# The input projection of two token groups by seven block products in place of eight

## The chip, the core and the metric

The kernel runs on one core of one Trainium2 chip. A core has TensorE (PE; matmuls into PSUM, with a weight load, PEld, ahead of each), VectorE (DVE), ScalarE (ACT), GpSimd (POOL) and SyncE (SP), which issues nearly all DMAs of this kernel. Each engine works through its own queue in order. The metric is device time in microseconds; the median of the runs before is 2421.81 us (2421.06 to 2422.79, three runs).

## The reference

One layer of a decoder step on 2048 prompt tokens and 64 sample tokens (8 sequences of 8), model width 1024, float32:

```
h    = rmsnorm(x, norm_mix_w)
rq, rk, rv, rg, hq, hf, hi, hg = split(h @ w_in)          # 8 parts of 4 heads x 128 columns
A: rq, rk rotated; retention with a fixed decay per head  (chunks, running 128x128 state)
B: f = lb + (1-lb)*sigmoid(hf);  k = 1-f;  q = silu(hq);  S_t = diag(f_t) S_(t-1) + k_t v_t^T;  o_t = S_t^T q_t
o    = concat(head_rmsnorm(o_A)*silu(rg), head_rmsnorm(o_B)*silu(hg))
x    = x + o @ w_out
x    = x + square(relu(rmsnorm(x, norm_ffn_w) @ w_up)) @ w_down       # width 4096
y    = rmsnorm(x, final_norm_w)
```

The outputs are y for both token sets and the final states of both head groups.

## The kernel before

The tokens are worked on in three groups (`GROUPS`): group one has the 64 sample tokens and 512 prompt tokens (576 columns, worked on in two pieces of 288), groups two and three have 768 prompt tokens each (two pieces of 384). For each group in turn the mixing runs (`mix`, then `out_proj`); after that the three groups go through the feed-forward (`ffn`).

Every float32 operand is held as two parts, `hi` (rounded to the fast matmul type) and `lo` (the rest), and a product is three matmuls: hi x hi, hi x lo, lo x hi. A weight tile is 128 x 1024. Loaded raw, it is cast on ACT into `hi` (L273), and DVE subtracts to get `lo` (L287, `second_part`). `weight` keeps a fixed number of tiles ahead of use (`self.ahead`, 2). There are `NPART` = 5 buffers for each part and `NRAW` = 4 raw ones. Group one's weights, from the fifth on, are also written out as parts (`keep`), and groups two and three load the two parts ("p" entries of `plan_stream`) in place of casting again.

Mixing takes one head of each kind at a time, four times a group. `project` makes the forget, query, rotary query and rotary key blocks by `proj`, with a weight block stationary and tokens moving: 8 blocks of the contraction, 3 part products, 2 pieces (L347). DVE and ACT take each result out of PSUM, scaled by the reciprocal norm. `values` makes values and gates of both kinds with 128 tokens stationary and 512 weight columns moving (L793), and holds four weight tiles at once. `mixer` then does the chunkwise recurrence of that head. It does not run its steps at once. It puts them on an agenda with due times in ticks (`at`, `later`); `proj` ticks once per part product, and `values` ticks too, so the mixer's steps of one head lie between the projection matmuls of the next. Weight sums of the feed-forward are made meanwhile by `plan_sums`, on its own tick list (`side`), eight sets in each of groups two and three, with raw tiles and DVE (L1401).

The feed-forward is already done by seven block products in place of eight (`PRODUCTS`, `T_SUMS`): a matrix product is cut into 2 x 2 blocks, and sums of weight blocks (S1 to S4, made ahead and kept in DRAM) and of activation blocks (T1 to T4) take the place of one product. `product` does one of them, 2 x 4 x 3 = 24 matmuls (through `matmul`, L1369), and `up` adds the results together from PSUM, with four two-bank PSUM tiles in turn (`two_banks`). The mixing stage has two such tiles (pool `pj`) and four single banks (`mm`).

Temporaries are 128 x 768 tiles from one pool (`get`, `NSLAB` = 43) and six more for loads (`load`). Tiles are handed out as their last readers finish. A scheduler orders each engine's instructions by due place and readiness, except where `keep_in_program_order` fixes it. A second, general form of the kernel (`fast` False) is built behind a branch and runs only if decays reach too far.

Of the kernel before, what the change touches and what calls it, by code (L numbers as in the profile page):

```python
# [15 lines left out]
P = 128  # L16
# [13 lines left out]
NSLAB = 43  # L30
NLD = 6
NRAW = 4
NPART = 5
# [26 lines left out]
N_KEPT = W_OUT0 + 4  # L60

# [13 lines left out]
PRODUCTS = (("A11", "B11"), ("S2", "T2"), ("A12", "B21"), ("S3", "T3"), ("S1", "T1"), ("A22", "T4"), ("S4", "B22"))  # L75
EARLY, LATE = (("A12", "B21"), ("S4", "B22")), (("S2", "T2"), ("S3", "T3"), ("S1", "T1"), ("A22", "T4"))
# [127 lines left out]
class Kernel:  # L204
    def __init__(self, tc, I, O, fast):
        self.tc, self.nc, self.I, self.O, self.fast = tc, tc.nc, I, O, fast
        self.tag = "f" if fast else "g"
        self.agenda, self.n_at, self.now = [], 0, 0
# [40 lines left out]
    def weight(self, i):  # L249
        n = len(self.stream)  # L250
        while self.w_next < min(i + 1 + self.ahead, n):
            j = self.w_next
            e = self.stream[j]
            if e[0] == "p":

                self.wts[j] = tuple(self.wp.tile([P, WT], F32R, tag=tag, name=tag, bufs=NPART) for tag in ("hi", "lo"))
# [3 lines left out]
                self.w_load = max(self.w_load, j + 1)  # L260
                continue
            while self.w_load <= j or j >= W_UQ0 and self.w_load <= j + 2 and self.w_load < n:
                if self.stream[self.w_load][0] == "p":
                    break
                k = self.w_load
                raw = self.raws[k] = self.wp.tile([P, WT], F32, tag="raw", name="raw", bufs=NRAW)
                e = self.stream[k]
                self.fetch(raw, self.sums[e[1]] if e[0] == "s" else self.I["w"][e[1]])
                self.w_load += 1
            raw = self.raws.pop(j)  # L270
            hi = self.wp.tile([P, WT], F32R, tag="hi", name="hi", bufs=NPART)
            lo = self.wp.tile([P, WT], F32R, tag="lo", name="lo", bufs=NPART)
            self.nc.scalar.copy(hi, raw)  # L273
            self.wts[j] = (hi, lo)
            self.second[j] = raw
            if j < 4:
                self.second_part(j)
            else:
                self.later(4, self.second_part, j)
# [3 lines left out]

    def second_part(self, j):
        if j in self.second:
# [3 lines left out]
    def plan_stream(self):  # L289
# [16 lines left out]
        mixing()  # L306
        mixing()
# [6 lines left out]
    def next_weight(self):  # L314
# [3 lines left out]
        if N_MADE <= i < N_KEPT:  # L318
# [5 lines left out]
    def keep(self, parts, kept):  # L324
        for part, k in zip(parts, kept):
            self.nc.sync.dma_start(k, part.bitcast(F32))

# [1661 lines left out]
```

## Time and profile before

| | us |
|---|---|
| median of the runs | 2421.81 |
| the profiled execution | 2421.02 |
| its span | 2419.2 |
| mixing of group one, from its first projection | 6.5 to 267.5 |
| mixing of group two / group three | 334 to 657 / 723 to 1046 |
| feed-forward | 1111 to the end |

The profile is of one execution. Its page gives busy times of each engine, the granted TensorE clock and DMA share in 40 slices, the chain of work that ended last, and groups of instructions by line. A table by stage gives, for each stretch, its length and the busy time of each engine. The chain of waits names, in order of time, what the next step waited for. The stage limits above are the times at which the line of the projection matmuls changes in the timeline.

### The profile page before, as it was taken

The page shows a single profiled execution, that of the slowest core. Times are in us where ns is not written, and L with a number is a line of the kernel's source. Part 1 is how long each engine was busy: PE and PEld are TensorE (multiplying, and loading weights), DVE is VectorE, ACT ScalarE, POOL GpSimd, SP SyncE. Part 2 cuts the span into 40 slices and gives each one's busy share as a digit, 9 for nine tenths or more (in the row PEclk, how much of TensorE's full clock was granted, in tenths as well). Part 3 has the DMA queues.
Part 4 walks back from the last instruction along what each step waited for, and adds up shares of the span by engine and source line. Part 5 has one row for each costly group of instructions (what it writes and reads, how often), then busy time and mean ns, then how long its engine had stood idle before and what let it go on. Part 6 is the DMA issues. An engine that isn't in the chain of part 4 may idle for free.

```text
span 2419.2 us, 37190 instructions
## 1 busy us (share of the span) xinstructions
PE 2399.0 (99%) x14650; PEld 2312.9 (96%) x14650; DVE 1597.4 (66%) x2014; ACT 1148.9 (47%) x1847; POOL 206.6 (9%) x230
## 2 busy tenths in 40 slices
PE   9999999999999999999999999999999999999998
PEld 8998898899899998899999999999999999999997
DVE  6555654443564443547868998766988887679886
ACT  6555543344543443435545555444544364445443
POOL 5222111211102101200000000000000000000000
PEclk9999999999999999999999999999999999999999
DMA  7777676556566655558768666766755557675542
GB/s 272 249 244 247 209 276 224 194 218 244 185 212 226 252 214 205 214 169 274 256 216 306 210 208 196 247 216 206 267 182 175 170 169 266 208 234 182 190 167 89
DMA packets 191966, 525.39 MB, mean 217 GB/s; under 512 B 21155, under 2 KB 62883, under 8 KB 191782
## 3 DMA queue, kind: packets, MB, share of 16 engines
q1 hardware_dynamic: 191638, 522.90, 63.0%
q8 instruction: 117, 1.92, 0.3%
q14 instruction: 67, 0.55, 0.1%
q10 hardware_dynamic: 144, 0.02, 0.0%
HBM read 389.14 MB, written 132.39 MB: 216 GB/s over the span
## 4 chain that ended last, share of the span: by engine, by line
PE 91%; DVE 3%; ACT 2%; issue 2%; POOL 1%; DMA 1%; DVEq 0%; ACTq 0%; POOLq 0%
PE pf L1369 27%; PE pj L1369 26%; PE pj L347 20%; PE pjv L793 11%; PE mm L1213 1%; PE mm L1215 1%; PE mm L1221 1%; PE mm L1358 1%; PE mm L990 1%; DVE slab L945 1%; PE mm L1143 1%; POOL slab L949 1%; PE mm L904 1%; DVE slab L974 0%; PE mm L838 0%
## 5 line engine op out<-in xcount | busy, mean ns | idle before, releaser
L273 ACT CAST hi<-raw 128x1024 fp32r<-128x1024 f32 x392 | 412.6, 1053 | 614.7 <-PE pf L1369 237.7
L1369 PE MATMUL pf<-slab,hi 128*128 128x384 f32 (+1 forms) x2768 | 652.0, 321 | 0.0
L1369 PE MATMUL pj<-slab,hi 128*128 128x384 f32 (+1 forms) x2608 | 617.8, 322 | 0.0
L287 DVE TENSOR_TENSOR lo<-raw,hi 128x1024 fp32r<-128x1024 f32 x392 | 481.7, 1230 | 127.0 <-ACT hi L273 122.5
L1369 PEld LDWEIGHTS pf<-slab,hi 128*128 128x128 f32 x2768 | 480.0, 188 | 0.1
L347 PE MATMUL pj<-slab,hi 128*128 128x384 f32 (+1 forms) x2304 | 477.3, 324 | 0.4 <-ACT hi L273 0.4
L1369 PEld LDWEIGHTS pj<-slab,hi 128*128 128x128 f32 x2608 | 453.6, 188 | 0.0
L1369 PE MATMUL pf<-slab,lo 128*128 128x384 f32 (+1 forms) x1384 | 443.1, 320 | 0.0
L1369 PE MATMUL pj<-slab,lo 128*128 128x384 f32 (+1 forms) x1304 | 418.9, 321 | 0.0
L347 PEld LDWEIGHTS pj<-slab,hi 128*128 128x128 f32 x2304 | 383.8, 188 | 4.1 <-issue 1.4
L793 PE MATMUL pjv<-hi,slab 128*128 128x512 f32 x1024 | 349.8, 402 | 0.0
L347 PE MATMUL pj<-slab,lo 128*128 128x384 f32 (+1 forms) x1152 | 281.5, 325 | 1.0 <-DVE lo L287 1.0
L1369 PEld LDWEIGHTS pf<-slab,lo 128*128 128x128 f32 x1384 | 260.1, 188 | 0.0
L1369 PEld LDWEIGHTS pj<-slab,lo 128*128 128x128 f32 x1304 | 245.0, 188 | 0.0
L793 PEld LDWEIGHTS pjv<-hi,slab 128*128 128x128 f32 x1024 | 192.6, 188 | 36.6
L793 PE MATMUL pjv<-lo,slab 128*128 128x512 f32 x512 | 200.8, 392 | 0.0
L347 PEld LDWEIGHTS pj<-slab,lo 128*128 128x128 f32 x1152 | 198.3, 188 | 1.5 <-DVE lo L287 1.5
L1460 ACT CAST slab<-slab 128x768 fp32r<-128x768 f32 (+1 forms) x192 | 145.7, 779 | 79.2 <-DVE slab L1471 53.9
L1464 DVE TENSOR_TENSOR slab<-slab 128x768 fp32r<-128x768 f32 (+1 forms) x192 | 166.4, 886 | 18.3 <-PE pf L1369 6.2
L793 PEld LDWEIGHTS pjv<-lo,slab 128*128 128x128 f32 x512 | 96.7, 189 | 15.8
L1401 DVE TENSOR_TENSOR raw<-raw 128x1024 f32<-128x1024 f32 x64 | 104.6, 1634 | 0.8
L1230 DVE SCALAR_TENSOR_TENSOR S<-S,mm 128x128 f32<-128x128 f32 x60 | 17.2, 286 | 111.7 <-PE mm L1221 102.2
(236 smaller groups left out, 2304.7 us busy)
## 6 DMA issues: line engine op xcount, KB each, us to landing
raw<-w SPq DMA_DIRECT2D x264, 512.0 KB, 4.5
slab<-fu SPq DMA_DIRECT2D x64, 384.0 KB, 5.1
fu<-ld SPq DMA_DIRECT2D x60, 384.0 KB, 4.1
ld<-x SPq DMA_DIRECT2D x32, 384.0 KB, 3.7
ld<-fin SPq DMA_DIRECT2D x28, 384.0 KB, 4.7
slab<-fu SPq DMA_DIRECT2D x32, 288.0 KB, 4.6
fu<-ld SPq DMA_DIRECT2D x30, 288.0 KB, 3.0
fres<-slab SPq DMA_DIRECT2D x16, 384.0 KB, 3.5
```

What stands on the lines that cost most here:

```text
L273: self.nc.scalar.copy(hi, raw)
L287: self.nc.vector.tensor_tensor(out=lo, in0=self.second.pop(j), in1=hi.bitcast(F32), op=ALU.subtract)
L347: self.nc.tensor.matmul(pj[:, i, :T2], w, a[:, c0:c1], start=j == 0 and q == 0, stop=j == n - 1 and q == 2)
L793: nc.tensor.matmul(dst, a[:, s:s + C], ww, start=kb == 0 and q == 0, stop=kb == KB - 1 and q == 2)
L904: nc.tensor.transpose(ps[:, j * P:(j + 1) * P], src[:, c], self.ident)
L945: nc.vector.tensor_tensor_scan(out=bb[:, c], data0=self.ones, data1=lf[:, c], initial=0.0, op0=ALU.mult, op1=ALU.add)
L949: nc.gpsimd.tensor_tensor(out=dd[:, n0:T].rearrange("p (n m) -> p n m", m=C), in0=b3, in1=b3[:, :, C // 2 - 1:C // 2].to_broadcast([P, n, ...
L990: nc.tensor.matmul(ps[:, j * P:(j + 1) * P], k[:, cols[c]], q[:, cols[c]], start=True, stop=True)
L1369: self.nc.tensor.matmul(*a, **k)
L1401: self.tc.keep_in_program_order(nc.vector.tensor_tensor(out=x[into], in0=x[a], in1=x[b], op=op))
L1460: self.nc.scalar.copy(hi[:, :g.T], B[name][:, :g.T])
L1464: self.nc.vector.tensor_tensor(out=lo[:, :g.T], in0=B[name][:, :g.T], in1=hi.bitcast(F32)[:, :g.T], op=ALU.subtract)
```

## The change

Group one and the feed-forward keep their matmuls. In groups two and three the input projection is done by seven block products for eight, twice per head:

- forget, query, rotary query and rotary key together are one 512-column output (`project_blocks`). Output columns are halved (forget and query / rotary query and key), as are the contraction and the tokens (384). Each of seven calls of `product` is 24 matmuls of 384 columns, weights stationary.
- values and gates together are another (`values_blocks`). Tokens are halved into trios of chunks, the output into values and gates. Each of seven calls of `product_t` is 3 x 4 x 3 = 36 matmuls of 256 columns, tokens stationary.

The sums of weight blocks for both are made during group one by `plan_in_sums`: 16 sets of four half tiles, summed on POOL, stored by DMA. `keep_blocks` writes group one's weight parts out in block form, for three of four blocks. `norm_blocks` takes the place of `norm_in` for groups two and three: it loads the activation blocks, weighs them on POOL, sums and splits them. Per head six weight tiles are loaded as kept parts and eight as raw sums, which are cast (`first_part`, five ticks later) and subtracted (`second_part`, nine ticks later). The fast form has 45 slabs, 6 raw tiles and 3 buffers of each part (`SIZES`); before, it was 43, 4 and 5. Group one's values are looped by weight tile (`values_direct`), so one tile at a time is held. Gate tiles are overwritten with the head outputs (`b["slabs"]`), and the outputs of the first three heads go to DRAM and back (`keep_heads`, `fetch_heads`).

```diff
+SIZES = {True: (45, 6, 3), False: (43, 4, 5)}
+FIRST = (("A11", "B11"), ("S4", "B22"), ("A12", "B21"), ("S2", "T2"), ("S3", "T3"), ("S1", "T1"), ("A22", "T4"))
 def weight(self, i):
...
+            if e[0] == "s" and j < self.n_sums:
+                self.later(5, self.first_part, j)
+                self.later(9, self.second_part, j)
+            else:
+                self.first_part(j)
...
+        def mixing_blocks():
+            for p in range(H):
+                for part in "PV":
+                    key = ("i", p, part)
+                    self.stream += [("s" if name[0] == "S" else "p", key + (name,)) for name, _ in (FIRST if part == "P" and not p else PRODUCTS)]
...
+    def plan_in_sums(self, start, each):
...
+        def make(x, name, a, op, b, into):
+            self.tc.keep_in_program_order(nc.gpsimd.tensor_tensor(out=x[into][:, :HALF], in0=x[a][:, :HALF], in1=x[b][:, :HALF], op=op))
...
+            if self.fast:
+                self.plan_in_sums(40, 40)
             self.mix(gs[0])
...
+    def norm_blocks(self, g):
...
+        for v, t0, t1 in ((0, 0, 40), (1, 84, 134)):
+            for j, name in enumerate(("B11", "B21", "B22", "B12")):
+                t = t0 + 7 * j
+                self.later(t, load, v, name)
+                self.later(t + 9, square, v, name)
+                self.later(t + 12, weigh, v, name)
+                if name != "B12":
+                    cut(t + 18, v, name)
+            for j, name in enumerate(("T3", "T2", "T1", "T4")):
+                self.later(t1 + 6 * j, self.block_sum, g, B[v], name)
+                cut(t1 + 6 * j + 4, v, name)
...
+    def project_blocks(self, g, p, b):
...
+        a = bank()
+        self.product(g, parts(a), "B11")
+        p1 = copied(a)
...
+            u = bank()
+            self.product(g, parts(u), "T2")
+            u2 = added(u, p1)
+        self.product(g, parts(a), "B21", False)
+        z = self.get()
+        nc.vector.tensor_tensor(out=b2(z), in0=a, in1=wide(g.rs, 0), op=ALU.mult)
+        gated(z, 0, False)
...
+        d = bank()
+        self.product(g, parts(d), "T3")
+        u3 = added(d, u2)
+        c = bank()
+        self.product(g, parts(c), "T1")
+        turned(added(c, u3), 1)
...
+        self.product(g, parts(d), "T4", False)
+        turned(added(d, u2), 0)
+        if p:
+            self.product(g, parts(c), "B22", False)
+            gated(added(c, u2), 1, True)
+
+    def product_t(self, g, ps, op, first=True):
+        hi, lo = self.next_weight()
+        for tb in range(TRIO):
+            for kb in range(KB // 2):
+                ah, al = (self.pair(g, s)[:, kb % 2, tb * C:(tb + 1) * C] for s in g.ops[kb // 2][op])
+                cols = slice(kb * 256, (kb + 1) * 256)
+                for j, (t, w) in enumerate(((ah, hi), (ah, lo), (al, hi))):
+
+                    self.nc.tensor.matmul(ps[:, tb * 256:(tb + 1) * 256], t, w[:, cols], start=first and kb == j == 0 and tb != 1,
+                                          stop=kb == KB // 2 - 1 and j == 2, skip_group_check=True)
+                self.tick()
...
+        if fast:
+            late = 13 if g.blocks else 0
...
+            at(4 + late, reaches)
+            at(15 + late, both_decays)
+            at(20 + late, both_decayed)
...
+            t = 92 if g.blocks else 96 if n0 else 84
+            outs(t)
```

`values_blocks` goes through the same seven products with `product_t` and takes each result out of PSUM in the same order; `gated` and `turned` are the gate and rotary steps on a result, partly on POOL.

More of the change, by code (lines that the diff above doesn't have):

```diff
@@ L282, in weight, with load_raws, first_part @@
         return self.wts[i]
+    def load_raws(self, j):
+        last = j if j < W_UQ0 else j + 2 if j >= self.n_sums else j + 1 if self.fast else j
+        if j < self.n_sums and self.stream[j][0] == "p" and not self.fast:
+            return
+        for k in range(j, min(last + 1, len(self.stream))):
+            e = self.stream[k]
+            if e[0] == "p" or k < self.w_load:
+                continue
+            raw = self.raws[k] = self.wp.tile([P, WT], F32, tag="raw", name="raw", bufs=self.n_raw)
+            self.fetch(raw, self.sums[e[1]] if e[0] == "s" else self.I["w"][e[1]])
+            self.w_load = k + 1
+    def first_part(self, j):
+        if j in self.first:
+            self.nc.scalar.copy(self.wts[j][0], self.first.pop(j))
     def second_part(self, j):
+        self.first_part(j)
         if j in self.second:
@@ L400, in build @@
             self.ahead = 2
-            self.wts, self.second, self.kept = {}, {}, {}
+            self.wts, self.first, self.second, self.kept = {}, {}, {}, {}
             self.blocks = deque()
```

356 lines of the change are left out of this document (312 added, 44 removed).

## The prediction

> **What bounds the kernel now.** I read the page first (busy shares, granted clock, chain), then the stage table, then the pace of matmuls inside each stage.
>
> ```profile
> span 2419.2 us, 37190 instructions
> PE 2399.0 (99%) x14650; PEld 2312.9 (96%) x14650; DVE 1597.4 (66%) x2014; ACT 1148.9 (47%) x1847; POOL 206.6 (9%) x230
> PEclk9999999999999999999999999999999999999999
> PE 91%; DVE 3%; ACT 2%; issue 2%; POOL 1%; DMA 1%; DVEq 0%; ACTq 0%; POOLq 0%
> ```
>
> TensorE is busy 99% of the span at full clock and carries 91% of the chain. Since a busy PE need not be at its peak, the stage table is checked next (columns: stretch, its length, busy us of PE, PEld, DVE, ACT, POOL, clock, DMA share, GB/s). Group one mixes until 267.5, groups two and three in 334:657 and 723:1046; the feed-forward starts at 1111.
>
> ```profile
> core 0: us, PE busy (x) PEld busy (x) DVE busy (x) ACT busy (x) POOL busy (x), PEclk, DMA share, GB/s
> 6.50:66.00 59.50, 57.14 (x341) 50.25 (x342) 39.27 (x49) 40.33 (x65) 30.82 (x36) 1.00 0.77 276
> 66.00:267.50 201.50, 201.06 (x1289) 179.52 (x1288) 105.32 (x196) 111.21 (x253) 49.06 (x66) 1.00 0.66 227
> 334.00:657.00 323.00, 321.50 (x1820) 294.68 (x1819) 139.11 (x208) 128.80 (x298) 55.43 (x50) 1.00 0.61 224
> 657.00:723.00 66.00, 66.00 (x397) 65.93 (x396) 43.37 (x57) 34.22 (x58) 4.04 (x4) 1.00 0.57 193
> 723.00:1046.00 323.00, 321.50 (x1819) 294.62 (x1818) 139.33 (x208) 128.91 (x298) 55.15 (x50) 1.00 0.61 223
> 1111.00:1470.00 359.00, 359.00 (x2693) 358.90 (x2692) 304.45 (x363) 192.94 (x239) 0.00 (x0) 1.00 0.74 244
> 1470.00:1938.00 468.00, 468.00 (x2704) 468.00 (x2703) 366.87 (x395) 219.95 (x252) 0.00 (x0) 1.00 0.63 205
> ```
>
> In both stages that the change rewrites, PE idles 1.5 us in 323. DVE stands at 43%, ACT at 40%, DMA at 61%. So time there is the sum of matmul durations, and a matmul taken away shortens the span, as long as what comes with it stays hidden.
>
> The matmuls concerned, by shape (L347 is the projection with weights stationary, and 768 of its 2304 belong to the output projection; L793 is the values and gates, a quarter of it group one's):
>
> ```profile
> L793 PE MATMUL pjv<-hi,slab 128*128 128x512 f32 x1024 | 349.8, 402 | 0.0
> L347 PE MATMUL pj<-slab,hi 128*128 128x384 f32 x1536 | 336.5, 337 | 0.0
> L793 PE MATMUL pjv<-lo,slab 128*128 128x512 f32 x512 | 200.8, 392 | 0.0
> L347 PE MATMUL pj<-slab,lo 128*128 128x384 f32 x768 | 197.6, 338 | 0.0
> ```
>
> The means (402, 337 ns) overlap, so the pace comes from unbroken runs: one stretch of the feed-forward (288 columns), two pieces and two head marks of the chain of waits (384 and 512 columns), and one run of the timeline (128 columns).
>
> ```profile
> 1197.30:1470.00 272.70, 272.70 (x2047) 1.00 0.72 237
> ```
> ```profile
> 378.77 0.91 PE mm L990 x6
> 396.15 6.83 PE pjv L793 x30
> 423.50 22.90 PE pj L347 x132
> 457.76 0.91 PE mm L990 x6
> ```
> ```profile
> 69.62 1.91 PE L838 MATMUL mm<-ld,slab 128*64 128x128 f32 x16
> ```
>
> 288 columns: 272.7/2047 = 133.2 ns. 384: 22.90/132 = 173.5. 512: 6.83/30 = 227.7. Slopes are 0.420 and 0.423 ns a column, so the three lie on one line of about 12 ns plus 0.42 a column. The 128-column run is off it at about 109 ns (1.91 us less one 0.27 us duration, over 15 steps). One head lasts 457.76 - 378.77 = 79.0 us.
>
> **The change, part by part.** *Forget to keys.* A head had 4 blocks x 8 x 3 x 2 = 192 matmuls of 384 columns and gets 7 x 24 = 168 of the same shape. 24 x 173.5 = 4.16 us a head, 8 heads: -33.3.
>
> *Values and gates.* 6 x 8 x 3 = 144 of 512 columns (32.8 us) become 7 x 36 = 252 of 256 columns. Nothing in the trace has 256 columns. The nearest rows are 288 (133 ns, upper end) and 128 (109 ns, lower end). The line gives 133.2 - 32 x 0.42 = 120 ns; I take it, since 288 lies on the line and is 32 columns away. 252 x 120 = 30.2, so -2.5 a head and -20.2 in all. At 133 the new form costs 33.5 (+0.8 a head, +6); at 109 it costs 27.5 (-42). PE in all: -53.5, between -27 and -75.
>
> The Trainium skill ("TensorE: Matmul & The Clock Gate", Back-to-back issue gap) gives columns/2.4 GHz + 2.5 ns, an estimate of 109 ns here, and by it the sum would be 22 us lower. The trace disagrees: 133.2, 173.5 and 227.7 against 122.5, 162.5 and 215.8, so the rows decide.
>
> *Group one: weight sums and kept blocks.* 16 sets add 64 POOL sums of 512 columns and 128 DMAs of 256 KB. POOL rows (the second at 512 columns):
>
> ```profile
> L975 POOL TENSOR_TENSOR slab<-slab 128x768 f32<-128x768 f32 x8 | 14.8, 1850 | 4.4 <-ACT slab L962 4.4
> L895 POOL TENSOR_TENSOR ld<-ld,slab 128x512 f32<-128x512 f32 x8 | 8.2, 1050 | 11.8 <-PE mm L838 8.9 <-DMA ret_so<-ld 3.0
> ```
>
> 64 x 1.05 = 67 us on a POOL busy 80 of 261: hidden. The bytes are tighter: 33.6 MB over 640 of 672 ticks (249 us) is +135 GB/s, and kept parts fall from 8 to 6 pairs of 1 MB a head (-32). 227 + 135 - 32 = 330, and the row's 227 at share 0.66 means 344 when full: 96%. At the start it is over: 276 + 135 + stores of the first four weights. Weights are fetched two ahead (some 13 us), which absorbs most. Cost 0 (cover holds) to 12 (the start's surplus of about 7 MB, 21 us of DMA time, less the 3 MB that the rest can make up); I take 3, near the cover.
>
> *Operands of groups two and three.* 14 splits for 8, 8 block sums, and 14 POOL products of 1.85 us, in out_proj where POOL is at 4 of 66 us and DVE at 43. Sums are read only from the fourth product on. Cost 0 to 5; 1.
>
> *Weight stream.* A head reads 6 kept pairs (1 MB each) and 8 sums (0.5 MB): 10.5 MB for 8.4. With the spilled heads that is about 13 MB a group more: 224 x 323 = 72 MB becomes 85 MB in 296 us, 287 GB/s, where 224/0.61 = 367 is full: 78%. Only 3 part buffers remain, so a pair is issued when the product three back ends, and has two products, 2 x 4.16 = 8.3 us bare (10.3 us with the mixer between). Landing times (us, last column) of those pairs now:
>
> ```profile
> lo<-fw11lo SPq DMA_DIRECT2D x2, 512.0 KB, 11.7
> hi<-fw20hi SPq DMA_DIRECT2D x2, 512.0 KB, 9.6
> lo<-fw19lo SPq DMA_DIRECT2D x2, 512.0 KB, 9.4
> hi<-fw28hi SPq DMA_DIRECT2D x2, 512.0 KB, 9.1
> hi<-fw12hi SPq DMA_DIRECT2D x2, 512.0 KB, 8.8
> lo<-fw27lo SPq DMA_DIRECT2D x2, 512.0 KB, 8.8
> lo<-fw5lo SPq DMA_DIRECT2D x2, 512.0 KB, 8.4
> hi<-fw6hi SPq DMA_DIRECT2D x2, 512.0 KB, 3.2
> ```
>
> Seven of 46 listed exceed 8.3 us, by 7.7 us together; two reads of 48 kept pairs would give about 8. On SP the waiting pair holds back sum loads, which have slack. Cost 0 to 16; I take 5, as most products have the mixer between.
>
> *Evacuations.* The DVE rows:
>
> ```profile
> L287 DVE TENSOR_TENSOR lo<-raw,hi 128x1024 fp32r<-128x1024 f32 x392 | 481.7, 1230 | 127.0 <-ACT hi L273 122.5 <-DMA raw<-fsd01S 2.9
> L690 DVE TENSOR_TENSOR slab<-pj,slab 128x768 f32<-128x768 f32 x16 | 15.3, 955 | 35.4 <-PE pj L347 35.4
> L754 DVE TENSOR_TENSOR slab<-slab 128x768 f32<-128x768 f32 x16 | 15.0, 940 | 3.9 <-POOL slab L753 3.9
> L974 DVE TENSOR_TENSOR slab<-slab 128x768 f32<-128x768 f32 x8 | 13.8, 1722 | 23.1 <-ACT slab L963 23.1
> ```
>
> A head gains 11 adds from PSUM (10.5 us), rotary in halves (3.9) and 8 second parts (9.8), and loses 7 operations (6.4): +17.8. DVE goes from 34 of 79 to 52 of 72 us, 72%. ACT gains 8 casts of about 1.05 and two copies: 31 to 41 us, 57%. Both stay below PE. But project_blocks and values_blocks turn over two PSUM pairs only: each product's pair is wanted again one product later, so an evacuation has 4.16 - 0.96 = 3.2 us of room, 112 times. The feed-forward has DVE at 78 to 85% without a PE wait, with four pairs. Cost 0 (as there) to 56 (each late by half a microsecond); I take 6, one hand-off in 18 late by a microsecond, since 72% is below the feed-forward's load.
>
> *Fewer part buffers in the feed-forward.* Five become three, so a cast starts when the product three back ends, not five. In group one a product lasts 24 x 0.133 = 3.2 us: two of them, less cast and second part (1.05 + 1.23), leave 4.1 us. Behind a waiting cast in ACT's queue stand copies out of PSUM, which wait no longer than one product's end. A late second part in the timeline, with its cast:
>
> ```profile
> 1451.18 1.05 ACT L273 CAST hi<-raw 128x1024 fp32r<-128x1024 f32 x1 [1.42 <-issue]
> 1458.35 2.35 DVE L287 TENSOR_TENSOR lo<-raw,hi 128x1024 fp32r<-128x1024 f32 x2
> ```
>
> 1458.35 - 1452.23 = 6.1 us of lag, 2 more than is left. This happens at the end of the stage, where DVE work bunches. Cost 0 to 10 (five weights 2 us late); 3. Groups two and three have 6.0 us of room: nothing.
>
> *Sum.* 2421.0 (the profiled execution: span 2419.2 and 1.8 around it) - 53.5 + 3 + 1 + 5 + 6 + 3 = 2385.5. The median of the runs is 0.8 above that execution: 2386.
>
> **The rivals.**
> 1. All cover holds, as in the stages above where PE never waits: 2421.8 - 53.5 = 2368. For it: the stage table. Against: three of the five covers are thinner than anything in this trace.
> 2. The 256-column pace is 133 ns, because a weight load per 256 columns binds: 26 us less gain, 2412. For it: loads double in number per column. Against: 109 ns in the 128-column run.
> 3. The pace is 109 ns: 2364. Against it: three points on one line.
> 4. Group one is paced by DMA: 12 for 3, 2395. For it: 96% of what the rows show.
> 5. Slower: DVE misses the PSUM hand-off. L974 takes 1722 ns where the same shape takes 940 (L754), and it runs beside a POOL operation of the same size (L975, 1850). The change puts more POOL work (gating, sums, weighing) beside DVE. A block of up to 0.9 us in front of the evacuations eats into the 3.2 us. It decides from 0.48 us lost per hand-off (53.5/112); at 0.6 us the time is 2421.8 - 53.5 + 67 + 12 of the other waits = 2447. Against it: POOL is busy 17% of these stages, so few hand-offs meet it.
>
> The Trainium skill ("SBUF — State Buffer", SBUF: two separate sides) has this as an exclusive lock: a DVE operation with two SBUF inputs and a GpSimd operation that reads SBUF block one another for the whole instruction. The trace agrees in kind (1722 against 940). By it PSUM-sourced adds, with one SBUF input, are delayed only by what stands ahead of them in the queue.
>
> **How the numbers follow.** Forecast 0.54, rival 1 0.12, rival 2 0.10, rival 3 0.04, rival 4 0.08, rival 5 0.12. A measurement of this kernel tells about 0.2% (5 us) from no change. Rival 5 is split 0.03 within that and 0.09 slower; the rest is faster, 0.88. The forecast's own range is 2370 to 2400. The range 2366 to 2414 takes in rivals 1, 2 and 4 for the most part and leaves out rival 3 and rival 5, with some of rival 2: about 0.81.
>
> **What would show it.** Right: heads of groups two and three about 72 to 74 us apart (79.0 now); 256-column runs at 120 ns; PE waits on DVE, on kept pairs and on PSUM adding up to 10 to 20 us. Wrong: a 256-column pace near 133; PE waits for `hi` or `lo` in every head; group one's mixing longer than 261 us; the feed-forward of group one longer than 359 us by more than 10.

## The result and the profile after

The changed kernel takes 2482.28 us (median of four runs, 2473.59 to 2487.27) against 2421.45 on the same chip: a ratio of 1.0246, 95% interval 1.0217 to 1.0275. It is slower by 61 us, where 35 us less were forecast. The profiled execution is one of 2482.16 us.

The head of its page, and the chain that ended last:

```profile
span 2480.4 us, 39533 instructions
PE 2377.4 (96%) x15322; PEld 2324.3 (94%) x15322; DVE 1784.7 (72%) x2168; ACT 1244.0 (50%) x1941; POOL 400.6 (16%) x348
PEclk9999999999999999999999999999999999999999
PE 73%; DVE 6%; ACT 3%; DMA 2%; POOL 2%; issue 2%; SPq 0%; DVEq 0%; POOLq 0%; ACTq 0%
```

PE falls from 99% to 96% of a longer span and from 91% to 73% of the chain. The time is no longer a sum of matmuls.

The stage table of the changed kernel (stretch, length, busy us of PE, PEld, DVE, ACT, POOL, clock, DMA share, GB/s). The rows are group one's mixing, the first output projection, group two's mixing, the second output projection, group three's mixing, and group one's feed-forward. A mixing stage ends with the group's last values or gates matmul, an output projection with the last of its 384 projection matmuls.

```profile
6.20:306.90 300.70, 272.20 (x1622) 235.77 (x1622) 158.68 (x235) 147.00 (x301) 167.91 (x166) 0.97 0.89 299
306.90:398.40 91.50, 71.34 (x491) 66.26 (x490) 67.72 (x89) 50.04 (x100) 32.55 (x22) 0.94 0.80 266
398.40:703.50 305.10, 287.83 (x2078) 284.16 (x2077) 199.47 (x262) 165.25 (x314) 82.36 (x63) 0.99 0.75 257
703.50:787.80 84.30, 78.77 (x475) 76.58 (x475) 65.71 (x80) 43.77 (x87) 34.73 (x19) 1.00 0.74 258
787.80:1095.70 307.90, 289.79 (x2078) 286.13 (x2078) 200.08 (x262) 165.65 (x316) 80.56 (x62) 0.98 0.74 255
1171.60:1530.60 359.00, 359.00 (x2693) 358.91 (x2692) 304.24 (x363) 192.64 (x239) 0.00 (x0) 1.00 0.75 244
```

The first five stages of the kernel before, by the same limits:

```profile
6.70:267.30 260.60, 258.00 (x1628) 229.59 (x1629) 144.22 (x243) 151.17 (x314) 79.88 (x102) 1.00 0.68 238
267.30:333.80 66.50, 64.64 (x486) 62.81 (x485) 49.77 (x75) 41.18 (x84) 9.76 (x9) 1.00 0.81 268
333.80:647.40 313.60, 312.10 (x1754) 285.32 (x1754) 135.10 (x198) 121.69 (x274) 55.23 (x49) 1.00 0.61 224
647.40:722.80 75.40, 75.40 (x462) 75.29 (x461) 47.38 (x67) 41.35 (x81) 4.24 (x5) 1.00 0.58 197
722.80:1036.50 313.70, 312.20 (x1754) 285.36 (x1753) 135.32 (x198) 121.85 (x275) 54.95 (x49) 1.00 0.60 223
```

So group one lost 40.1 us, the first output projection 25.0, the second 8.8; groups two and three won 8.5 and 5.8; the feed-forward of group one is unchanged. Group one and the output projections keep their matmuls. Most of the loss lies in stages whose arithmetic did not change.

The matmuls themselves did what the sum said. One run of the new form in the timeline of the changed kernel (start, length, engine, line), its first row and the row that follows 22 matmuls later:

```profile
581.28 0.28 PE L1031 MATMUL pj<-hi,slab 128*128 128x256 f32 x1
...
583.90 0.28 PE L1031 MATMUL pj<-lo,slab 128*128 128x256 f32 x1
```

That is 2.62/22 = 119 ns, where 120 were forecast.

What PE waited for over the whole span (waiting tile and line, releaser, us in total, times, longest):

```profile
PE pj L441 <- DVE slab L1789: 11.5, 6, 5.0
PE pj L1031 <- DVE slab L1046: 10.2, 8, 1.7
PE mm L1391 <- DVE slab L1765: 8.3, 2, 4.1
PE pj L441 <- DVE slab L1834: 7.0, 6, 1.7
PE pj L1031 <- DVE slab L955: 4.8, 4, 1.5
```

L1789 and L1834 are the additions that free the output projection's PSUM pairs, L1046 and L955 those of the block products, and L1765 makes second parts of the head outputs (`cut_heads`). None of the waits is long, and DVE idles a quarter of the span. In group one the waits of the other engines show more. SP's queue first, then ACT, both in group one:

```profile
SPq L404 <- POOL slab L398: 53.4, 28, 6.4
SPq L362 <- ACT hi L296: 8.9, 4, 4.0
```
```profile
ACT hi L296 <- DMA raw<-w: 28.4, 8, 7.2
```

SP, which issues every weight load, stood for 53.4 us in front of the store of a weight sum (L404) that POOL had not made yet (L398). ACT waited 28.4 us for weights. That the one causes the other is not shown by these rows: in the kernel before, SP stood 83 us at the stores of kept parts (L326, group one), and PE idled only 2.6 us there. The experiments decide it.

```profile
SPq L326 <- ACT hi L273: 37.5, 11, 4.8
...
SPq L326 <- ACT slab L864: 31.1, 4, 8.8
SPq L326 <- DVE lo L287: 14.7, 14, 2.0
```

### The profile page after: what moved, and what is told of

The parts are those of the page before. It is cut to its first block, busy times and chain, and to the rows that moved or that the text cites. A ratio compares the mean times of both kernels' runs of the same rounds, so it can differ in the third digit from the quotient of the medians.

```text
span 2480.4 us, 39533 instructions
## 1 busy us (share of the span) xinstructions
PE 2377.4 (96%) x15322; PEld 2324.3 (94%) x15322; DVE 1784.7 (72%) x2168; ACT 1244.0 (50%) x1941; POOL 400.6 (16%) x348
## 4 chain that ended last, share of the span: by engine, by line
PE 73%; DVE 6%; ACT 3%; DMA 2%; POOL 2%; issue 2%; SPq 0%; DVEq 0%; POOLq 0%; ACTq 0%
PE pj L1774 32%; PE pf L1774 27%; PE pj L1031 6%; PE pj L441 5%; DVE lo L302 1%; PE mm L1616 1%; DVE slab L1869 1%; DMA raw<-w 1%; PE mm L1614 1%; POOL slab L1350 1%; PE mm L1622 1%; PE mm L1391 1%; DVE slab L979 1%; DVE slab L1375 0%; DMA lo<-fki0PA12lo 0%
## 5 line engine op out<-in xcount | busy, mean ns | idle before, releaser
L1774 PE MATMUL pj<-slab,hi 128*128 128x384 f32 (+1 forms) x3504 | 854.1, 326 | 1.3 <-ACT slab L950 1.3
L302 DVE TENSOR_TENSOR lo<-raw,hi 128x1024 fp32r<-128x1024 f32 x448 | 566.4, 1264 | 178.6 <-ACT hi L296 175.5
L1774 PE MATMUL pj<-slab,lo 128*128 128x384 f32 (+1 forms) x1752 | 571.0, 326 | 0.5 <-DMA lo<-fki0PA12lo 0.5
L1031 PE MATMUL pj<-hi,slab 128*128 128x256 f32 x1344 | 267.7, 291 | 18.4 <-DVE slab L1046 10.2
L441 PE MATMUL pj<-slab,hi 128*128 128x288 f32 (+1 forms) x1280 | 259.0, 320 | 25.6 <-DVE slab L1789 11.5
L1031 PEld LDWEIGHTS pj<-hi,slab 128*128 128x128 f32 x1344 | 219.0, 194 | 21.3 <-issue 11.4
L1869 DVE TENSOR_TENSOR slab<-slab 128x768 fp32r<-128x768 f32 (+1 forms) x208 | 184.7, 905 | 11.2 <-ACT slab L1865 4.4
L1031 PE MATMUL pj<-lo,slab 128*128 128x256 f32 x672 | 191.6, 285 | 0.0
L441 PE MATMUL pj<-slab,lo 128*128 128x288 f32 (+1 forms) x640 | 152.2, 317 | 0.6 <-DVE lo L302 0.6
L1031 PEld LDWEIGHTS pj<-lo,slab 128*128 128x128 f32 x672 | 130.5, 194 | 0.0
L398 POOL TENSOR_TENSOR slab<-slab 128x512 f32<-128x512 f32 x64 | 88.4, 1382 | 32.3 <-DMA slab<-w 30.1
```

Of the source, the lines that this page charges most:

```text
L302: self.nc.vector.tensor_tensor(out=lo, in0=self.second.pop(j), in1=hi.bitcast(F32), op=ALU.subtract)
L398: self.tc.keep_in_program_order(nc.gpsimd.tensor_tensor(out=x[into][:, :HALF], in0=x[a][:, :HALF], in1=x[b][:, :HALF], op=op))
L441: self.nc.tensor.matmul(pj[:, i, :T2], w, a[:, c0:c1], start=j == 0 and q == 0, stop=j == n - 1 and q == 2)
L1031: self.nc.tensor.matmul(ps[:, tb * 256:(tb + 1) * 256], t, w[:, cols], start=first and kb == j == 0 and tb != 1, stop=kb == KB // 2 - 1 an ...
L1774: self.nc.tensor.matmul(*a, **k)
L1869: self.nc.vector.tensor_tensor(out=lo[:, :g.T], in0=B[name][:, :g.T], in1=hi.bitcast(F32)[:, :g.T], op=ALU.subtract)
```

## The experiments

The totals below are of one run each ("before" and "changed" are the profiled executions). The changed kernel's own four runs lie 14 us apart, so stages are compared rather than totals. A stage whose work an edit leaves alone came out within 298.8 to 305.0 us (group one, seven runs), 90.2 to 94.5 (first output projection, three) and 304.3 to 307.2 (group two, ten). Group one is G1, the output projections P1 and P2; all in us.

| run | total | G1 | P1 | G2 | P2 | G3 |
|---|---|---|---|---|---|---|
| before | 2421.0 | 260.6 | 66.5 | 313.6 | 75.4 | 313.7 |
| changed | 2482.2 | 300.7 | 91.5 | 305.1 | 84.2 | 307.9 |
| e1 no sums | 2444.3 | 269.7 | 83.7 | 306.5 | 84.3 | 306.4 |
| e2 sums not made, but moved | 2460.5 | 278.1 | 90.9 | 306.0 | 84.3 | 307.8 |
| e3 weighing off POOL | 2475.7 | 298.8 | 90.7 | 305.6 | 80.6 | 307.8 |
| e4 no second parts of sums | 2459.3 | 305.0 | 90.2 | 293.8 | 83.0 | 294.2 |
| e5 other load tiles | 2481.8 | 302.8 | 91.6 | 304.9 | 84.3 | 305.3 |
| e6 sums on DVE | 2484.3 | 297.7 | 96.4 | 307.2 | 84.3 | 306.4 |
| e8 three PSUM pairs | 2514.6 | 325.5 | 95.9 | 305.9 | 84.0 | 309.8 |
| e9 heads cut later | 2471.2 | 300.5 | 94.5 | 298.5 | 83.7 | 301.3 |
| e10 stores by POOL | 2531.9 | 357.1 | 85.2 | 304.7 | 84.3 | 307.9 |
| e11 second parts of operands on ACT | 2468.6 | 299.7 | 86.7 | 306.2 | 78.2 | 305.3 |
| e12 stores later | 2466.4 | 282.3 | 95.2 | 304.3 | 84.3 | 307.8 |
| e13 operand steps apart | 2471.2 | 301.1 | 83.3 | 305.6 | 80.0 | 308.3 |
| e14 = e3+e9+e12+e13 | 2432.4 | 283.7 | 78.5 | 299.8 | 77.7 | 300.2 |
| e15 = e14, sums 60 apart | 2457.9 | 289.9 | 71.6 | 324.3 | 79.6 | 300.2 |
| e16 = e15, weighing on POOL | 2457.9 | 286.9 | 77.6 | 321.6 | 78.8 | 300.4 |
| e17 = e14, stores 36 behind | 2438.7 | 286.7 | 80.6 | 299.8 | 78.7 | 300.1 |
| e18 = e17, sums 46 apart | 2453.1 | 287.2 | 82.5 | 311.3 | 77.7 | 301.7 |
| e19 = e14, no sums | 2412.8 | 270.2 | 71.1 | 299.7 | 77.7 | 300.2 |

### Group one: the sums, their making, and SP's queue

**e1**, no sums at all, and **e2**, everything of the sums but the POOL instruction:

```diff
-                self.plan_in_sums(40, 40)          # e1
-            ... nc.gpsimd.tensor_tensor(out=x[into][:, :HALF], ...)   # e2, in make
```

> The changed kernel without the 16 sets of weight sums in group one: no loads, no POOL sums, no stores; groups two and three load a raw weight tile where they loaded a sum, so the outputs are not the reference's, and the lower bounds are raised to keep decays finite. Changed kernel: mixing of group one 300.8 us, its output projection 91.5, mixing of groups two and three 305 and 308, 2482 in all. Theory 1 (the sums cost group one its time, by POOL work or by DMA bytes): group one 262 to 270, output projection 70 to 85, total 2425 to 2445. Theory 2 (three part buffers, values looped by weight tile and few free slabs cost it): group one stays at 290 to 301, total above 2465. Groups two and three unchanged within 5 us in both.

> The changed kernel with the loads and stores of the 16 sets, but without the 64 POOL operations that make the sums (blocks are stored as loaded, so outputs are not the reference's; lower bounds raised as before). Theory 1a (POOL: its queue, and DVE held up beside it): group one falls from 300.8 to 262 to 272 as without sums. Theory 1b (DMA bytes): group one stays at 288 to 301, since bytes are the same. Half and half would give about 282.

The sums cost 31.0 us of G1's 40.1 and 7.8 of P1. With their loads and stores kept, G1 is 278.1: 22.6 of the 31 come with the making and the waits for it, though DMA is busier without them (G1's row of e2: share 0.94, 324 GB/s):

```profile
6.20:284.30 278.10, 264.74 (x1624) 231.01 (x1623) 142.78 (x237) 147.84 (x302) 79.32 (x102) 0.99 0.94 324
```

**e6**: is it POOL blocking DVE?

```diff
-nc.gpsimd.tensor_tensor(out=x[into][:, :HALF], ...)
+nc.vector.tensor_tensor(out=x[into][:, :HALF], ...)
```

> The changed kernel with the 64 weight sums of group one made by DVE in place of POOL, same loads and stores; the output is unchanged. Theory 1a sharpened (it is POOL's queue and the time that POOL and DVE block each other, not the sums as such): DVE has 159 of 301 us busy there and takes about 0.65 us for each sum, 42 us in all; group one 300.7 falls to 278 to 286 (278.1 was measured with no sums made), total 2460 to 2468. Rival (any engine's time for the sums costs the same, through lateness of weight parts): group one stays at 292 to 301.

G1 stays at 297.7. The second parts of weights are back at their duration of before (mean 1294 ns; 1517 in the changed kernel, 1293 before), but DVE has the 48.4 us of the sums on top, and the run does not show how far the one hides the other. Whichever engine makes them, SP waits for it at the same store:

```profile
SPq L404 <- DVE slab L398: 46.9, 26, 5.8
```

That row gave the theory that the queue, not the work, costs the time. **e10** gave the stores to POOL's queue, **e12** left them on SP and put them 12 to 13 steps later:

```diff
-nc.sync.dma_start(self.sums[key + (name,)]...            # e10
+nc.gpsimd.dma_start(self.sums[key + (name,)]...
-((30, "S1"), (34, "S3"), (39, "S2"), (44, "S4"))         # e12
+((42, "S1"), (47, "S3"), (52, "S2"), (57, "S4"))
```

> The stores of the group-one block sums are issued by POOL, which makes the sums, instead of by SP; everything else is unchanged. Theory 7 (SP's queue is in order: a sum's store stands at its head until POOL has made the sum, 53.4 us in 28 waits in group one, and the weight loads behind it come late, so that ACT's casts and the PSUM evacuations behind them are late): group one falls from 300.7 us to about 278, where it stood with the same loads and stores and no sums made; ACT's waits for weight loads (27.9 us in 8) shrink to a few us; the whole comes to about 2460. The rival (the making itself costs the time: POOL's sums lock out DVE, or their engine time delays the chain) expects group one within 4 us of 300.7 and the whole at 2478 or more.

> The stores of the group-one block sums stay on SP but are issued 12 to 13 planner steps later (20 steps behind their sum instead of 7 or 8); nothing else is changed. Theory 7 (SP's in-order queue stands at a store until POOL has made the sum, 53.4 us in group one, and the weight loads behind it come late): SP's waits for POOL's sums fall below 10 us, ACT's waits for weight loads (27.9 us) below 12, group one falls from 300.7 us to 278 to 285 and the whole to about 2462. The rival (POOL is late with the sums for a reason of its own, and the chain through POOL, not SP, sets group one): SP's waits for sums shrink as well, but group one stays within 5 us of 300.7 and the whole at 2477 or more.

e10 missed and could not decide: it moved the block to another queue. POOL stood at many of its own stores, up to 5.9 us at one, and the mixer waited for POOL (waits of e10 in its first 300 us):

```profile
...
PE mm L1391 <- POOL slab L1376: 29.7, 3, 11.1
...
POOL fsi2PS L404 <- issue: 17.7, 6, 4.8
```

e12 did: the same POOL work, bytes and slabs, and G1 is 282.3 us. SP's waits for sums in G1 are down to

```profile
SPq L404 <- POOL slab L398: 12.6, 12, 4.4
```

so about 18 us of G1's loss (18.4, one run, against a stage that varies by 6) are the place of 64 stores in SP's order. P1 rose to 95.2 in that run, so that the whole gained 16. The remaining 13.5 us of the sums (G1 of e14 against e19) are their traffic and making, not told apart further.

### The output projections: DVE's queue

**e3** took the weighing (L789) and square sums (L783) of the operands off POOL. **e5** took the residual's input out of the load tiles that the operands also use.

```diff
-nc.gpsimd.tensor_tensor(out=y, in0=y, in1=self.vec[...]..., op=ALU.mult)     # e3
+for i in range(2): nc.scalar.activation(y[:, i], y[:, i], AF.Copy, scale=...)
-            x = self.x_block(g, n)                                           # e5
+            x = self.wp.tile([P, WT], F32, tag="raw", ...)
```

> The changed kernel with the weighing of the activation blocks on ACT (two operations of 384 columns) and the adds of squares on DVE, so norm_blocks has no POOL products ahead of its splits. Theory 3 (POOL products hold up DVE splits, which hold up the PSUM adds of the output projection): output projection of group one 91.5 to 75 or less, of group two 84.3 to 78, the total 15 to 25 lower, 2457 to 2467. Rival (backlog of weight sums and DMAs, or slabs): output projections within 4 us of the changed kernel's, total 2478 to 2486.

> The changed kernel with the residual's x blocks in the output projection loaded into raw weight tiles (six, of which the output projection needs few) in place of the six load tiles, which norm_blocks holds four at a time. Theory 5 (the residual's x waits for a load tile, DVE's add for x, and TensorE for the add): output projection of group one 91.5 falls to 76 or less, of group two 84.3 to 78 or less, total 2455 to 2468. Rival (DVE or DMA is what is late there): both within 4 us of the changed kernel's, total above 2474.

Neither moved P1 (90.7 and 91.6); e3 won 3.6 us in P2. The timeline of the changed kernel shows what PE waits for in its longest stop there (start, length, engine, line, in brackets the idle time before and its releaser):

```profile
346.07 0.81 ACT L1865 CAST slab<-ld 128x768 fp32r<-128x768 f32 x1
346.24 1.80 POOL L783 TENSOR_TENSOR slab<-slab 128x768 f32<-128x768 f32 x1 [0.62 <-ACT slab L781]
...
346.99 1.87 DVE L1869 TENSOR_TENSOR slab<-ld,slab 128x768 fp32r<-128x768 f32 x1 [2.50 <-ACT slab L1865]
...
348.78 0.74 DVE L1789 TENSOR_TENSOR slab<-pj,ld 128x576 f32<-128x576 f32 x1
...
349.67 1.30 PE L441 MATMUL pj<-slab,hi 128*128 128x288 f32 x4 [5.04 <-DVE slab L1789]
```

DVE idled 2.5 us in front of an operand's subtraction (L1869) whose cast was not done, then needed 1.87 us for it, beside a POOL operation; the addition that PE waits for (L1789) stood behind. The six subtractions of this form in P1, in the changed kernel, in e3 (a line lower in that kernel) and in e13:

```profile
L1869 DVE TENSOR_TENSOR slab<-ld,slab 128x768 fp32r<-128x768 f32 x6 | 12.3, 2057 | 2.6 <-ACT slab L1865 2.5
```
```profile
L1870 DVE TENSOR_TENSOR slab<-ld,slab 128x768 fp32r<-128x768 f32 x6 | 5.7, 951 | 0.0
```
```profile
L1869 DVE TENSOR_TENSOR slab<-ld,slab 128x768 fp32r<-128x768 f32 x6 | 6.0, 997 | 0.0
```

So without POOL's work beside them they take half the time. In e3 DVE got the square sums instead (5.7 us), and its work in P1 hardly fell (65.70 for 67.72): e3 does not show that POOL's work is harmless there.

Two reasons are possible for the stop: the amount of DVE work, stretched or not, or its place in the queue. **e11** took the 14 subtractions of each group off DVE, **e13** left all work and set the steps further apart:

```diff
-nc.vector.tensor_tensor(out=lo, ..., op=ALU.subtract)     # e11, operands of groups two and three
+nc.scalar.copy(lo, B[name])
-for v, t0, t1 in ((0, 0, 40), (1, 84, 134)): t = t0 + 7 * j   # e13
+for v, t0, t1 in ((0, 0, 50), (1, 100, 150)): t = t0 + 9 * j
-zip((0, 4), self.halve(...))
+zip((0, 10), self.halve(...))
```

> In the preparation of the operands of groups two and three (14 blocks beside each of the first two output projections) the second part is made by a copy on ACT in place of DVE's subtraction, so the second part of each operand holds another number than it should; slabs, loads and matmuls are the same. Theory 8 (the first output projection is slower by 25 us because the 14 splits and 6 block sums, 27 us against 15 before, fill DVE: 67.7 us of work in a stage that took 66.5): without 21.5 us of them on DVE the first output projection falls from 91.5 to 75 us or less, the second from 84.2 to about 78, the whole to about 2460. The rival (slab tiles and SP's queue set the time there: SP waits 21 us for slabs that DVE's additions give back) expects the first output projection at 88 us or more.

> In the preparation of the operands of groups two and three, planned beside the first two output projections, the steps are set further apart: 9 planner steps from block to block instead of 6 or 7, 10 from the cast of a block to the subtraction behind it instead of 4, 8 from a block sum to its cast instead of 4; the work is the same. Theory 8 in its second form (DVE's queue is in order: a subtraction that waits 2.5 us for ACT's cast, or a sum that waits for POOL, holds the residual additions that free the projection's PSUM buffers; PE waited 10.6 us for those additions in 5 waits): the first output projection falls from 91.5 us to 80 or less, the second from 84.2 to 78 or less, the whole to about 2463. The rival (DVE's amount of work, 67.7 us in a stage that took 66.5, sets it, whatever its order): both stay within 4 us of 91.5 and 84.2.

Both helped P1 by less than expected, 4.8 and 8.2 us; P2 gained 6.0 and 4.2. In e13 PE's waits for L1789 in P1 are 2.2 us for 10.6, with a DVE work of

```profile
307.20:390.50 83.30, 70.55 (x491) 65.96 (x490) 55.10 (x83) 46.37 (x98) 31.34 (x22) 0.96 0.80 273
```

where the changed kernel had 67.72 in the stage. Five operations of about a microsecond moved on into G2, and the six subtractions above no longer meet POOL's work, so e13 changes amount and order at once. So does e11: the subtractions that waited for casts went together with their work. Both runs point to DVE's queue; whether amount or order weighs more stays open.

### Groups two and three

**e4** left out the second parts of the sum weights (32 subtractions of 128x1024 a group), **e8** gave the block products a third PSUM pair from the mixer's, and **e9** put the reading back and cutting of the first heads' outputs later:

```diff
+                self.wts[j] = (hi, hi)                          # e4, sum weights of groups two and three
-tc.tile_pool(name="pj", bufs=2, ...)   pm: bufs=4              # e8
+tc.tile_pool(name="pj", bufs=3, ...)   pm: bufs=2
-self.later((16, 34, 60)[q], self.cut_heads, g, q)              # e9
+self.later((52, 64, 76)[q], self.cut_heads, g, q)
```

> The changed kernel without the second parts of the eight summed weight tiles per head (the third matmul of each reads the first part again, so outputs are not the reference's; lower bounds raised). This takes 64 DVE operations of 1.23 us, 9.8 us a head, out of groups two and three and nothing else. Theory 4 (DVE's load makes PSUM hand-offs late): mixing of groups two and three 305 and 308 fall to 288 to 296 each, total 2450 to 2470. Rival (operations held up beside POOL, or the order in DVE's queue, not its load): they fall by less than 5 us each.

> The changed kernel with three two-bank PSUM tiles for the products in place of two, at the cost of two of the four single banks of the mixer (and one two-bank tile less in the feed-forward's other pool, so that the eight banks hold). Theory 4b (two pairs leave a product's evacuation one product of room): the PE waits for the adds and copies of project_blocks and values_blocks, about 20 us over groups two and three, fall below 6. Groups two and three gain 5 to 10 us each if the mixer does well with two banks; if the mixer's steps then wait for banks, waits before the scores, outputs and states grow and eat the gain. Rival (the evacuations are late by more than one product, since DVE's queue is behind): the waits for adds stay above 14 us.

> The changed kernel with the fetching and cutting of the first three heads in groups two and three put 52, 64 and 76 ticks into the last head's values in place of 16, 34 and 60, behind the mixer's decays and scores. Theory 6 (the cut's DVE operations stand ahead of the last head's decayed keys in DVE's queue; TensorE waits 4 us for the scores and drops to half clock): waits of the scores for the cut, 8.3 us in the two groups, go to below 2, and the two half-clock windows of 6.8 us behind them go; groups two and three 4 to 7 us shorter each, total 2468 to 2475. Rival (the cut then is late for the output projection): output projections of groups two and three grow by as much.

e4: G2 293.8 and G3 294.2, 11.3 and 13.7 us less, with DVE at 157 us of the stage for 199. So DVE's load there costs PE time although DVE was busy only 65% of the stage. (The edit also frees buffers for weight parts; PE's waits for loads were 0.5 us in G2, so little can come from that.) In e8 the waits for L1046 and L955 went, and G2 and G3 stayed where they were (305.9 and 309.8); the mixer, with two PSUM tiles fewer, waited instead, and G1 lost 25 us (waits of e8 over the span):

```profile
PE mm L1391 <- DVE slab L1375: 14.2, 5, 4.0
PE mm L1763 <- DVE slab L1765: 13.0, 7, 4.1
```

A third pair at the mixer's cost wins nothing; whether one without that cost would is not shown.

e9 won 6.6 us in each group, more than the 8.3 us of waits on L1765 that it took away in both together. Its row of G2 shows why: PE idles 4.4 us less than in the changed kernel, and its matmuls take 2.4 us less, at a clock of 1.00 (last section).

```profile
401.70:700.10 298.40, 285.47 (x2077) 281.56 (x2077) 202.45 (x262) 164.64 (x313) 81.68 (x63) 1.00 0.76 263
```

e4's G2 runs at 1.00 too, so its gain and e9's overlap and may not be added.

### All together

> Four changes in one: sum stores 12 to 13 steps later, the operand steps set further apart, the fetching and cutting of heads later in groups two and three, and the weighing and square sums of the operands on ACT and DVE instead of POOL. If the causes are separate, the gains of the single runs add: group one 281, first output projection 81, group two 298.5, second output projection 78, group three 301 us, in all about 2435. If the stages only pass one delay on (what is won in one place waits in the next), less than half of the 45 us is won: 2458 or more.

> As the run of the four changes together, but no block sums are made in group one: they are neither loaded nor stored, and groups two and three load a whole weight block in the place of each sum (the same bytes), so that their products are of other numbers. What the sums still cost after their stores were moved is the difference. If only they keep the kernel above the one before: group one 268 us or less, the first output projection 74 or less, the whole 2405 to 2412. If the hand-offs of the block products and the kept blocks weigh as much, group one stays at 275 or more and the whole above 2420.

e14 is 2432.4: the single gains add up (44 us by their sum, 50 measured). It stays 12 us above the kernel before, which is less than the changed kernel's own runs lie apart. Without the sums (e19) it is 2412.8, 8 us below. So the sums still cost 19.6 us after their stores were moved (13.5 in G1, 7.4 in P1), and that is more than the 8 us that e19 keeps of the 54 that the matmuls should save. The other 45 are lost even there, some 13 in each of G2 and G3.

Four runs tried to lower that further: the 16 sets of sums 60 steps apart instead of 40 (**e15**; **e16** also with the weighing on POOL), the stores 36 steps behind their sums (**e17**), and that with the sets 46 apart (**e18**).

> As the run of the four changes together, and the 32 sets of block sums are planned 60 steps apart instead of 40, so that they run on past group one, through the first output projection and into group two, whose heads need them later. Theory 9 (the bytes of the sums cost group one the 8 to 9 us that stay when no sum is made, since its DMA engines are 93 to 94% busy): group one falls to 275 or less, the first output projection rises by at most 3 us, group two by at most 3, in all about 2430. The rival (the sums cost wherever they run): what group one wins, the later stages lose, and the whole is within 3 us of the run of the four changes.

> As the run with the sums 60 steps apart, but the weighing and the square sums of the operands stay on POOL. If POOL's sums and its weighing collide beside the first output projection (sums now run there too), this is 5 us or more slower than with them on ACT and DVE; if DVE's and ACT's load is what counts there, it is the faster of the two.

> As the run of the four changes together, with the sums' stores 36 steps behind their sums instead of 20. If SP's order is still part of what group one loses, SP's waits for sums (12.8 us) vanish and group one falls from 283.7 us to 276 to 280, the whole to 2425 to 2429. If what is left is the traffic of the sums and kept blocks, group one stays within 2 us and the whole within 3 us of 2432.4.

> As the run with the stores 36 steps behind, and the sets of sums 46 steps apart instead of 40, so that they end within the first output projection. At 60 steps apart group one did not become faster (289.9 us), the first output projection did (71.6), and group two lost 24. If group two's loss came from sums that still ran there, this has the first output projection at 75 or less without a loss in group two (300), in all 2420 to 2428; if any thinning disturbs group one, it is slower than the run with the stores 36 steps behind.

None did. In e15 P1 fell to 71.6 us, but G1 rose to 289.9 although its DMA share fell from 0.92 to 0.83, and G2 to 324.3, of which 12.2 us are one wait of PE for the first kept pair. e16 has the same total, with P1 6.0 us longer and G1 and G2 shorter: where POOL weighs shifts time between stages and wins none. e18 has the longer G2 as well (311.3), and P1 at 82.5. e17 took nearly all of SP's waits for sums away (3.0 us in G1) and G1 did not fall (286.7), so no more is to be had from SP's order beyond 20 steps, and theory 9 (bytes alone) fell with e15. What the 13.5 us in G1 consist of stays open, and so does why thinning the sums out lengthens G2.

## Why the prediction was wrong

The forecast and the measured time are 96 us apart. Three terms make it up: 45 in group one's sums and kept blocks, 25 in the operands, 28 in groups two and three (39 measured there, against 6 and 5 in the sum). The feed-forward's 3 us, which were not lost, go off.

**Right.** The matmul term: -53.5 by the sum. By the counts of the pages there are 192 matmuls of 384 columns and 1152 of 512 fewer, and 2016 of 256 more; at 173.5, 227.7 and the measured 119.1 ns that is -55.5. The 256-column pace was 119 ns for 120, so rivals 2 and 3 are out. The feed-forward's term of 3 us measured 0 (359.0 in both). What failed is the condition in "a matmul taken away shortens the span, as long as what comes with it stays hidden": it did not stay hidden.

**Wrong: "Group one: weight sums and kept blocks ... 64 x 1.05 = 67 us on a POOL busy 80 of 261: hidden ... I take 3" (0 to 12).** It measured 40 us in G1 and 8 in P1, and "group one's mixing longer than 261 us", a sign of being wrong that the prediction names, came true with 300.7. The step asked whether POOL had time and whether the DMA engines had bytes to spare, and both had (POOL busy 168 of 301 us, DMA share 0.89). It did not ask what stands behind a store that waits for its data on SP's queue. e12 shows 18 us of it to be that; e1 and e12 leave 13 for traffic and making, and 9 for the kept blocks, three part buffers and the values' new order, which no run took apart. Rival 4 (12 us by DMA) named the stage, not the mechanism.

**Wrong: "Operands of groups two and three ... Cost 0 to 5; 1".** P1 and P2 lost 25.0 and 8.8, of which the sums account for 7.8 in P1. "POOL is at 4 of 66 us and DVE at 43" is the row of the second output projection; the first had POOL at 9.8 and DVE at 49.8 of 66.5. There 18 us were added to DVE's work, 6.6 of them because six subtractions took twice as long beside POOL, and 67.7 is as much as the whole stage had lasted. At the stop shown above, the addition that frees a PSUM pair stood behind a subtraction that waited for ACT's cast. e11 and e13 recover parts; with e3's and e13's edits and no sums (e19) P1 is 71.1 and P2 77.7. A third PSUM pair did not help P1 (e8: 95.9).

**Mis-sized: "Evacuations ... Cost 0 to 56; I take 6".** Against the sum's matmul gain of 26.8 us a group, G2 and G3 fell short by 18.3 and 21.0, 39 in all and within the bounds. By the stage tables PE idles 17.3 and 18.1 us there for 1.5 before (32 us more), and its matmuls take 7 us longer at the lower clock. The choice of 6 leaned on the feed-forward, which runs DVE at 78 to 85% without a wait. That row has four PSUM pairs and no mixer; the new stage has two pairs and a mixer that needs DVE too. Two edits show a part each: e4 (-25 without the second parts) and e9 (-13 with the heads cut later); they overlap. That the number of pairs matters is not shown. The heads of group two follow each other in 75 to 77 us, for 72 to 74 forecast.

**Weight stream, 5 us:** PE waited 0.5 us for kept pairs in the whole span. The term was not needed.

**Rival 5** had the right sign, but not from where it looked. PE's waits for the additions that empty the block products' PSUM pairs (L1046 and L955) come to 15.0 us over 112 hand-offs, 0.13 us each, where it needed 0.48. DVE operations did stretch beside POOL (second parts of weights in G1: mean 1517 ns, 1293 before; the subtractions of P1: 2057 ns, 951 in e3). The exclusive lock of the Trainium skill ("SBUF — State Buffer", SBUF: two separate sides) agrees with these durations. What they cost stays open: e12 keeps the stretch in G1 (1506 ns) and G1 falls to 282.3; e6 and e3 remove it and leave G1 and P1 where they were, but give DVE other work (48.4 and 5.7 us).

## What to carry to other kernels

Engine shares tell whether work fits, not whether it is harmless: a store that waits for its producer stops every load behind it on the same queue, so issue it well after the producer is done, and give each issued instruction of a side task a place at which its operands are surely ready. A long wait on that queue is a hint only; move the store and see. Where a change takes one matmul in eight away, cost the sums that replace it as queue positions on SP and DVE. And check a borrowed cover ("as in the feed-forward") for what is different in the stage that borrows it.

## What the runs showed of the hardware

Short stops of PE cost more than their length. The stage table of the changed kernel around the 4.1 us wait for L1765 in G2 (678.08 to 682.22), in three stretches:

```profile
677.50:680.90 3.40, 0.58 (x5) 0.37 (x4) 2.06 (x2) 3.40 (x9) 1.81 (x1) 1.00 0.95 289
681.00:687.70 6.70, 5.48 (x26) 5.51 (x27) 6.25 (x9) 1.75 (x3) 0.00 (x0) 0.50 0.62 219
687.80:691.20 3.40, 3.40 (x31) 3.40 (x30) 2.17 (x3) 0.00 (x0) 0.00 (x0) 1.00 0.55 201
```

The granted clock is 0.50 for the 6.7 us that follow 3.4 us with 0.58 us of matmuls in them, and 1.00 after that. The clock records of the changed kernel hold ten such stretches before its last microseconds, six of 3.4 us and four of 6.8, which lengthened the matmuls in them by about 20 us (half of the PE time in them); the kernel before has none. The 3.4 us ahead of each of the ten hold 0 to 1.8 us of matmuls. The Trainium skill ("TensorE: Matmul & The Clock Gate", What's actually happening) gives a free-running window of 3413 ns after which an idle array is set to half clock. The trace agrees in length and clock; here the window before the drop was not idle but 17% busy. So a wait of 4.1 us, with half of the 5.48 us of matmuls behind it, cost G2 near 7, which fits what e9 won.
